# Two buffers of their own for the second quarter (b12) of the MLP's seven-product rounds

## The chip, the cores and the metric

The kernel runs on one core of one Trainium2 chip. The metric is the device time of one execution in microseconds. Three runs of the kernel before took 2303.08, 2305.74 and 2306.23 us; their median, 2305.74 us, is the time that the change is compared with.

## The reference

A decoder trunk of two layers over 256 tokens of width 2048, all in float32. Layer 0 mixes tokens with multi-head latent attention, layer 1 with a Mamba-2 scan; each mixer is followed by the same MLP, which is where the change is:

```python
def squared_relu_mlp(h, w_in, w_out):
    u = jax.nn.relu(h @ w_in)
    return (u * u) @ w_out

# in reference(), for each of the two layers
x = x + mix
h = rms_norm(x, mlp_norm_g[i])
x = x + squared_relu_mlp(h, mlp_w_in[i], mlp_w_out[i])
```

`w_in` is 2048 x 8192 and `w_out` 8192 x 2048, so each MLP reads 128 MB of weights.

## The kernel before

**Splitting.** A float32 weight is multiplied as a sum of two parts. Every piece of weights, 128 partitions x 1024 numbers (512 KB), is loaded into a raw buffer (`L85`, issued by SP). ScalarE copies it to a rounded high part `wh` (`L102`), VectorE subtracts that from the raw piece to give the low part `wl` (`L103`). TensorE multiplies high by high, low (of the activations) by high and high by low (`L615`, `L616`, `L619`). There are four `wh` and four `wl` buffers, so splitting runs at most a few units ahead of TensorE. A unit is one such piece with its products; units are numbered in the order in which TensorE consumes them, and the tile names carry that number (`wraw207`, `wl198`).

**Rounds.** The hidden width of an MLP is worked off in eight steps of 1024 columns. In steps 1 to 7 (the rounds of this text, seven in each MLP), `h @ w_in` for the step is done as a product of 2 x 2 blocks with seven products instead of eight: M1, N7, N5, N6, N4, M2, N3. The inner dimension of a block is walked in four pieces d = 0 to 3. For each d, three quarters of weights are loaded, b11 into the pool `rx`, b12 and b22 into the pool `raw`, and VectorE combines them in place (`L183`):

```python
if name == "N7":
    add("b22", "b12", "b22")
    out = halves("b22")
    ...
if name == "N5" and d not in LATE5:
    add("b12", "b11", "b12")
    return halves("b12")
if name == "N6":
    add("b11", "b11", "b22")
    out = halves("b11")
...
loads = {"M1": lambda: [load("b11", "rx", (0, 0))],
         "N7": lambda: [load("b12", B12, (0, 1)), load("b22", "raw", (1, 1))],
```

So a b12 buffer is held from its load, through the add of N7, until the split of N5. After N6 a DMA issued by GpSimd adds a further quarter onto b11 in place (`L199`). M2 and N3 load the quarter b21 or b22 again as plain pieces.

**Output.** The squared hidden columns of a round are multiplied by `w_out` in the next round, in blocks of 512 output columns with four units each (loads from `mo`). Such a block collects in a pair of PSUM banks (`yp`); at its end VectorE adds the two banks to the residual stream (`add_residual`, `L436`), and only then may the next block's first product write those banks.

**What sets the order.** TensorE's order is written out by a planner (`plan`, `merged`), which mixes the products of a round with the output units of the round before; the planner is not changed. Loads run six units ahead of TensorE inside the rounds and splits three (`self.flow.ahead`). The instructions of VectorE, ScalarE, GpSimd and SP are put into their queues by the framework's scheduler, which places each where its own estimate of durations has it start; each queue then runs strictly in that order, so an instruction that waits holds up what stands behind it. A raw load waits until the buffer that it takes has been read for the last time. Of the six `raw` buffers, a round's b12 pieces take one each while they are held.

Of the kernel before, what the change touches and what calls it, by code (L numbers as in the profile page):

```python
# [169 lines left out]
def seven(layer, p, src):  # L170
# [9 lines left out]
    def unit(flow, name, d):  # L180
# [22 lines left out]
        def load(k, pool, q):  # L203
            st[k] = Load(pool, quarter(d, *q))
            return st[k]

        loads = {"M1": lambda: [load("b11", "rx", (0, 0))],
                 "N7": lambda: [load("b12", B12, (0, 1)), load("b22", "raw", (1, 1))],
                 "M2": lambda: [load("M2", "raw", (1, 0))], "N3": lambda: [load("N3", "raw", (1, 1))]}
# [5 lines left out]
class Trunk:  # L215
# [294 lines left out]
    def mlp(self, layer, gain):  # L510
        with ExitStack() as ctx:
            mp = ctx.enter_context(self.tc.tile_pool(name="mlp", bufs=1, reuse_waits="tile"))
            for name, n in (("rx", 4), ("ry", 1)):
                self.flow.pools[name] = ctx.enter_context(self.tc.tile_pool(name=name, bufs=n, reuse_waits="tile"))
            self.flow.ahead = (4, 3)
            self.mlp_body(mp, layer, gain)
# [883 lines left out]
             "x7", "z5", "z6", "o2a", "z7", "o2b", "o3"]  # L1400


B12 = "raw"
WARM = 9
LATE5 = ()
TR = (10, 8, 7, 7, 5)
# [66 lines left out]
def sequence(d):  # L1473
# [23 lines left out]
    def mlp(i):  # L1497
# [9 lines left out]
        for nb in range(4):  # L1507
            for q in range(2):
                add(("mo", i, 7, nb, q), mo[14 + q, nb])

    mlp(0)
    col = lambda name, i: {"z": 0, "x": 8, "B": 16, "C": 18}[name] + i
    si = lambda name, i: [add(("si", name, i, q), d["si"][q, col(name, i)]) for q in range(4)]
    so = lambda k, nb: add(("so", k, nb), d["so"][k, nb])
    for step in SSM_ORDER:
# [8 lines left out]
        else:  # L1524
            for pair in ((0, 1), (2, 3)):
                for k in (6, 7):
                    for nb in pair:
                        so(k, nb)
    mlp(1)
    return seq  # L1530

# [78 lines left out]
```

## Time and profile before

| | |
|---|---|
| median of three runs | 2305.74 us |
| the profiled execution | 2303.41 us, of which the span 2301.6 us |
| TensorE busy | 2281.3 us (99%) |
| VectorE busy | 1897.7 us (82%) |
| ScalarE busy | 1391.8 us (60%) |
| HBM read | 529.65 MB, 233 GB/s read and written over the span |
| 512 KB loads into `raw` from `w_in` (`mi`), from `w_out` (`mo`) | 256 and 256, median 5.4 and 5.3 us to landing |

The profile is of one execution. Its timeline gives start, duration, engine, line, operation, tiles and, in brackets, the idle time before an instruction with what ended it; rows of equal instructions that follow each other are merged (x3). Its table of stretches gives, for each, the length and then the busy time of TensorE's matmuls, its weight loads, VectorE, ScalarE and GpSimd with their counts, the granted TensorE clock, the share of the time in which the DMA engines were busy, and GB/s. Its list of waits gives who waited for whom: total us, times, longest. Of a DMA, "to landing" is the time from its issue until its data had landed. The first MLP lies at about 275 to 925 us, the second at 1625 to 2275 us.

### The profile page before, as it was taken

Reading aid. Unit: us, or ns where it says so; the run is one execution under the profiler, and the core shown is the slowest. Engines: PE = TensorE matmul, PEld = TensorE weight load, DVE = VectorE, ACT = ScalarE, POOL = GpSimd, SP = SyncE. Lnnn points to the kernel's source line nnn. Section 1 sums busy time; section 2 is a strip of 40 time slices with the busy share of each in tenths; the row PEclk is TensorE's granted clock in tenths of the full one; section 3 lists DMA queues with packets and bytes.
Section 4 is the critical chain, followed back from the end, with each engine's and each line's share of the span. In section 5 each row is a group of like instructions: output and inputs, shape, how many; then the busy total and the mean of one; then the engine's idle time right before and its main releaser. Section 6 shows DMA issues by size and latency. Waiting matters only on the chain.

```text
span 2301.6 us, 30974 instructions
## 1 busy us (share of the span) xinstructions
PE 2281.3 (99%) x10929; PEld 1889.6 (82%) x10929; DVE 1897.7 (82%) x2290; ACT 1391.8 (60%) x1947; POOL 276.4 (12%) x315
## 2 busy tenths in 40 slices
PE   9999999999999999999999999999999999999999
PEld 7888888878878778888888888888888877878887
DVE  7786797888898888677899688677979889889884
ACT  7775566566566566564666645545666656666663
POOL 1440000000000000100133213121000000000000
PEclk9999999999999999999999999999999999999999
DMA  8545678888888878767878788767788888888874
GB/s 316 169 154 168 213 228 270 256 251 256 263 248 261 260 230 262 228 205 243 277 280 278 250 269 270 221 222 226 222 254 245 257 262 241 260 270 246 258 239 156
DMA packets 167709, 557.18 MB, mean 242 GB/s; under 512 B 19041, under 2 KB 28193, under 8 KB 166529
## 3 DMA queue, kind: packets, MB, share of 16 engines
q1 hardware_dynamic: 151264, 502.44, 66.8%
q0 software_dynamic: 13888, 48.49, 9.8%
q10 hardware_dynamic: 2400, 4.27, 0.5%
q8 instruction: 86, 1.41, 0.2%
q14 instruction: 71, 0.57, 0.1%
HBM read 529.65 MB, written 6.41 MB: 233 GB/s over the span
## 4 chain that ended last, share of the span: by engine, by line
PE 96%; DMA 2%; DVE 1%; issue 1%; ACT 0%; POOL 0%; DVEq 0%; SPq 0%; ACTq 0%
PE acc L339 13%; PE acc L340 13%; PE acc L343 13%; PE yp L615 9%; PE yp L619 9%; PE yp L616 9%; PE st L615 7%; PE st L616 7%; PE st L619 7%; DMA wraw<-mi 1%; PE sm L324 1%; PE sm L322 1%; PE y L1311 1%; PE acc L615 1%; PE acc L616 1%; PE acc L619 1%
## 5 line engine op out<-in xcount | busy, mean ns | idle before, releaser
L102 ACT ACTIVATE wh<-wraw 128x1024 fp32r<-128x1024 f32 (+1 forms) x818 | 857.8, 1054 | 604.3 <-PE acc L340 275.0
L103 DVE TENSOR_TENSOR wl<-wraw,wh 128x1024 fp32r<-128x1024 f32 (+1 forms) x818 | 984.9, 1221 | 238.0 <-ACT wh L102 225.6
L615 PE MATMUL yp<-wh,k 128*128 128x512 f32 x896 | 351.7, 393 | 12.7 <-DVE x L436 12.6
L616 PE MATMUL yp<-wh,k 128*128 128x512 f32 x896 | 349.8, 390 | 0.0
L339 PE MATMUL acc<-wh,xt 128*128 128x512 f32 x704 | 279.5, 397 | 0.5 <-ACT wh L102 0.5
L340 PE MATMUL acc<-wh,xt 128*128 128x512 f32 x704 | 274.8, 390 | 0.0
L102 ACT ACTIVATE wh<-wrx 128x1024 fp32r<-128x1024 f32 x168 | 177.7, 1060 | 136.8 <-PE yp L616 101.6
L619 PE MATMUL yp<-wl,k 128*128 128x512 f32 x896 | 239.9, 389 | 1.1 <-DVE wl L103 1.1
L103 DVE TENSOR_TENSOR wl<-wrx,wh 128x1024 fp32r<-128x1024 f32 x168 | 204.9, 1221 | 25.6 <-ACT wh L102 25.0
L615 PEld LDWEIGHTS yp<-wh,k 128*128 128x128 f32 x896 | 168.6, 188 | 53.6 <-issue 11.0
L619 PEld LDWEIGHTS yp<-wl,k 128*128 128x128 f32 x896 | 168.3, 188 | 36.6 <-DVE wl L103 1.5
L616 PEld LDWEIGHTS yp<-wh,k 128*128 128x128 f32 x896 | 168.8, 188 | 34.2
L339 PE MATMUL acc<-wh,k 128*128 128x512 f32 x496 | 196.5, 396 | 0.0
L340 PE MATMUL acc<-wh,k 128*128 128x512 f32 x496 | 193.3, 390 | 0.0
L343 PE MATMUL acc<-wl,xt 128*128 128x512 f32 x704 | 188.3, 389 | 0.0
L615 PE MATMUL st<-wh,xt 128*128 128x512 f32 x448 | 177.7, 397 | 0.0
L616 PE MATMUL st<-wh,xt 128*128 128x512 f32 x448 | 174.8, 390 | 0.0
L339 PEld LDWEIGHTS acc<-wh,xt 128*128 128x128 f32 x704 | 132.6, 188 | 29.2 <-ACT wh L102 1.4
L340 PEld LDWEIGHTS acc<-wh,xt 128*128 128x128 f32 x704 | 132.4, 188 | 28.5 <-issue 1.2
L343 PEld LDWEIGHTS acc<-wl,xt 128*128 128x128 f32 x704 | 132.2, 188 | 27.7
L619 PE MATMUL st<-wl,xt 128*128 128x512 f32 x448 | 138.0, 389 | 0.0
L199 POOL DMA_DIRECT2D wrx<-mi x56 | 49.2, 878 | 733.7 <-DVE wl L103 537.1
(319 smaller groups left out, 3464.1 us busy)
## 6 DMA issues: line engine op xcount, KB each, us to landing
wraw<-mi SPq DMA_DIRECT2D x256, 512.0 KB, 5.4
wraw<-mo SPq DMA_DIRECT2D x256, 512.0 KB, 5.3
wraw<-si SPq DMA_DIRECT2D x160, 512.0 KB, 5.2
wraw<-so SPq DMA_DIRECT2D x64, 512.0 KB, 5.5
wrx<-mi SPq DMA_DIRECT2D x56, 512.0 KB, 5.5
wrx<-mi POOLq DMA_DIRECT2D x56, 512.0 KB, 8.1
wraw<-wo SPq DMA_DIRECT2D x32, 512.0 KB, 3.9
taps<-xD SPq DMA_DIRECT2D x16, 768.0 KB, 8.2
```

The lines of the kernel that those rows point to most:

```text
L102: self.last = nc.scalar.activation(h[:, v], raw[:, v], AF.Copy)
L103: self.last_lo = nc.vector.tensor_tensor(lo[:, v], raw[:, v], h[:, v].bitcast(F32), ALU.subtract)
L199: nc.gpsimd.dma_start(st["b11"].tile, quarter(d, 1, 0), accum_op=ALU.add)
L322: self.nc.tensor.transpose(b.bitcast(F32R)[:, v], words[:, v], self.ident_r)
L324: self.nc.tensor.transpose(b[:, v], src[:, v], self.ident)
L339: nc.tensor.matmul(accs[t][:, :n], ah, wh[:, q, :], start=first and kt + q == 0, stop=False)
L340: nc.tensor.matmul(accs[t][:, :n], al, wh[:, q, :], start=False, stop=False)
L343: nc.tensor.matmul(accs[t][:, :n], lhs(kt + q, t)[0], wl[:, q, :], start=False, stop=en and q == nk - 1)
L615: nc.tensor.matmul(b, ah, half(h, q), start=first and q == 0, stop=False, skip_group_check=more)
L616: nc.tensor.matmul(b, al, half(h, q), start=False, stop=False, skip_group_check=more)
L619: nc.tensor.matmul(b, lhs(2 * kt + q, t)[0], half(lo, q), start=False, stop=last and q == 1, skip_group_check=more)
L1311: nc.tensor.matmul(y[t][c, o], part(t)[:, c], xg[g][t][:, o], start=True, stop=True)
```

## The change

A pool `rb` of two buffers of 128 x 1024 float32 (4 KB in each partition, so 8 KB more in all) is opened beside `rx` and `ry` for each MLP, and b12 is loaded into it. The six `raw` buffers serve all else as before.

```diff
@@ def mlp(self, layer, gain):
-            for name, n in (("rx", 4), ("ry", 1)):
+            for name, n in (("rx", 4), ("ry", 1), ("rb", 2)):
                 self.flow.pools[name] = ctx.enter_context(self.tc.tile_pool(name=name, bufs=n, reuse_waits="tile"))
             self.flow.ahead = (4, 3)
             self.mlp_body(mp, layer, gain)
@@
-B12 = "raw"
+B12 = "rb"
```

No instruction is added or removed. TensorE's and GpSimd's orders stay as they are; SP's, VectorE's and, in a few rows, ScalarE's change.

SP in round 3 of the first MLP, the loads around those of unit 207 (N7 of d = 3; `mi0` is the first MLP's `w_in`, `mo0` its `w_out`). Before:

```order
L85 DMA wraw198_4965<-mi0 128x1024
L85 DMA wraw198_4967<-mi0 128x1024
L85 DMA wraw199_4985<-mo0 128x1024
L85 DMA wraw202_5027<-mo0 128x1024
L85 DMA wraw203_5039<-mo0 128x1024
L85 DMA wraw204_5052<-mo0 128x1024
L85 DMA wrx227_5422<-mi0 128x1024
L85 DMA wraw207_5096<-mi0 128x1024
L85 DMA wraw207_5098<-mi0 128x1024
L85 DMA wraw210_5144<-mo0 128x1024
```

With the change:

```order
L85 DMA wraw198_4970<-mi0 128x1024
L85 DMA wrb198_4968<-mi0 128x1024
L85 DMA wraw199_4988<-mo0 128x1024
L85 DMA wraw202_5030<-mo0 128x1024
L85 DMA wraw203_5042<-mo0 128x1024
L85 DMA wrb207_5099<-mi0 128x1024
L85 DMA wraw204_5055<-mo0 128x1024
L85 DMA wraw207_5101<-mi0 128x1024
L85 DMA wrx227_5425<-mi0 128x1024
L85 DMA wraw210_5147<-mo0 128x1024
```

Both loads of 207 now stand ahead of that of `wrx227`, b12's also ahead of 204's. The load of 207's b22 takes, with the change, the buffer of 190's b22, whose last reader is the add for N6 of d = 1 (`wrx189<-wrx189,wraw190`); before, it took the buffer of 199, whose last reader is the split `wl199`.

VectorE in the same round, from split 197 to the residual adds (`x00` and `x10` are the residual stream's tiles). Before:

```order
L103 TENSOR_TENSOR wl197_5000<-wrx197_4947,wh197_4999 128x1024
L183 TENSOR_TENSOR wrx197_4947<-wrx197_4947,wraw198_4967 128x1024
L103 TENSOR_TENSOR wl198_5018<-wraw198_4967,wh198_5017 128x1024
L103 TENSOR_TENSOR wl199_5030<-wraw199_4985,wh199_5029 128x1024
L103 TENSOR_TENSOR wl200_5043<-wraw198_4965,wh200_5042 128x1024
L103 TENSOR_TENSOR wl201_5056<-wrx197_4947,wh201_5055 128x1024
L103 TENSOR_TENSOR wl202_5067<-wraw202_5027,wh202_5066 128x1024
L183 TENSOR_TENSOR wraw207_5098<-wraw207_5096,wraw207_5098 128x1024
L436 TENSOR_TENSOR x00_142<-yp_509_4945,x00_142 128x512
L436 TENSOR_TENSOR x10_146<-yp_510_4946,x10_146 128x512
```

With the change:

```order
L103 TENSOR_TENSOR wl197_5003<-wrx197_4950,wh197_5002 128x1024
L183 TENSOR_TENSOR wraw207_5101<-wrb207_5099,wraw207_5101 128x1024
L103 TENSOR_TENSOR wl198_5021<-wraw198_4970,wh198_5020 128x1024
L183 TENSOR_TENSOR wrx197_4950<-wrx197_4950,wraw198_4970 128x1024
L103 TENSOR_TENSOR wl199_5033<-wraw199_4988,wh199_5032 128x1024
L103 TENSOR_TENSOR wl200_5046<-wrb198_4968,wh200_5045 128x1024
L103 TENSOR_TENSOR wl201_5059<-wrx197_4950,wh201_5058 128x1024
L103 TENSOR_TENSOR wl202_5070<-wraw202_5030,wh202_5069 128x1024
L183 TENSOR_TENSOR wrb207_5099<-wrx206_5087,wrb207_5099 128x1024
L436 TENSOR_TENSOR x00_142<-yp_509_4948,x00_142 128x512
L436 TENSOR_TENSOR x10_146<-yp_510_4949,x10_146 128x512
```

The add for N7 of 207 moved from behind split 202 to behind split 197, and the add for N5 of the same piece from behind the residual adds to ahead of them. Rounds 4 to 6, and 2 in its last piece, change in the same way, in both MLPs; in rounds 3 to 6 the adds of d = 0, 1 and 2 keep their places.

VectorE in round 2, from split 135 (unit 140 is N7 of d = 0). Before:

```order
L103 TENSOR_TENSOR wl135_3999<-wraw135_3956,wh135_3998 128x1024
L436 TENSOR_TENSOR x02_144<-yp_466_3893,x02_144 128x512
L436 TENSOR_TENSOR x12_148<-yp_467_3894,x12_148 128x512
L300 TENSOR_TENSOR k4_464_3890<-sm_470_4016,k4_463_3889 128x4x128
L103 TENSOR_TENSOR wl136_4026<-wraw136_3968,wh136_4025 128x1024
L103 TENSOR_TENSOR wl137_4040<-wraw137_3980,wh137_4039 128x1024
L103 TENSOR_TENSOR wl138_4052<-wraw138_3996,wh138_4051 128x1024
L103 TENSOR_TENSOR wl139_4062<-wrx139_4023,wh139_4061 128x1024
L623 TENSOR_TENSOR s2_455_3774<-st_441_3377,s2_455_3774 128x512
L183 TENSOR_TENSOR wraw140_4037<-wraw140_4035,wraw140_4037 128x1024
```

With the change:

```order
L103 TENSOR_TENSOR wl135_4002<-wraw135_3959,wh135_4001 128x1024
L183 TENSOR_TENSOR wraw140_4040<-wrb140_4038,wraw140_4040 128x1024
L436 TENSOR_TENSOR x02_144<-yp_466_3896,x02_144 128x512
L436 TENSOR_TENSOR x12_148<-yp_467_3897,x12_148 128x512
L300 TENSOR_TENSOR k4_464_3893<-sm_470_4019,k4_463_3892 128x4x128
L103 TENSOR_TENSOR wl136_4029<-wraw136_3971,wh136_4028 128x1024
```

The add for N7 of 140 moved ahead of the residual adds and of splits 136 to 139.

## The prediction, as it went on record

> **What bounds the kernel now.** I read the page first, then the busy time of the two MLPs, then who waited for whom, then one round of the MLP engine by engine.
>
> ```profile
> PE 2281.3 (99%) x10929; PEld 1889.6 (82%) x10929; DVE 1897.7 (82%) x2290; ACT 1391.8 (60%) x1947; POOL 276.4 (12%) x315
> ```
> ```profile
> 275.00:925.00 650.00, 641.91 (x2897) 528.03 (x2896) 568.48 (x554) 407.20 (x441) 40.52 (x57) 1.00 0.83 252
> 925.00:1625.00 700.00, 700.00 (x3623) 577.89 (x3622) 553.63 (x742) 393.42 (x620) 129.97 (x90) 1.00 0.75 246
> 1625.00:2275.00 650.00, 643.94 (x2896) 529.71 (x2895) 566.47 (x548) 406.05 (x436) 37.59 (x52) 1.00 0.83 251
> ```
> ```profile
> PE yp L615 <- DVE x L436: 12.6, 8, 2.2
> PE yp L619 <- DVE wl L103: 1.1, 1, 1.1
> PE sm L322 <- DVE k L300: 0.4, 1, 0.4
> ...
> DVE wraw L183 <- DMA wraw<-mi: 50.9, 29, 3.7
> ```
>
> TensorE is busy 99% of the span, so no edit that leaves its matmuls alone can win more than its idle time. That idle time lies in the two MLPs, 650 - 641.91 = 8.1 us and 650 - 643.94 = 6.1 us; the SSM between them has none. The waits say how it arises: eight times, 12.6 us in all, the first matmul of an output block waited for the residual add (L436) that empties its bank; VectorE in turn stood 50.9 us, 29 times, at an add of raw weights (L183) whose load had not landed.
>
> Round 3 shows the link. VectorE's timeline, then TensorE's:
>
> ```profile
> 496.87 1.22 DVE L183 TENSOR_TENSOR wrx<-wrx,wraw 128x1024 f32<-128x1024 f32 x1
> ...
> 502.55 1.22 DVE L103 TENSOR_TENSOR wl<-wrx,wh 128x1024 fp32r<-128x1024 f32 x1
> 503.81 1.22 DVE L183 TENSOR_TENSOR wrx<-wrx,wraw 128x1024 f32<-128x1024 f32 x1
> 504.95 3.49 DVE L103 TENSOR_TENSOR wl<-wraw,wh 128x1024 fp32r<-128x1024 f32 x3
> ...
> 509.49 1.22 DVE L103 TENSOR_TENSOR wl<-wraw,wh 128x1024 fp32r<-128x1024 f32 x1
> 514.21 1.22 DVE L183 TENSOR_TENSOR wraw<-wraw,wraw 128x1024 f32<-128x1024 f32 x1 [3.50 <-DMA wraw<-mi]
> 515.35 1.28 DVE L436 TENSOR_TENSOR x<-yp,x 128x512 f32<-128x512 f32 x2
> ```
> ```profile
> 513.39 0.61 PE L619 MATMUL st<-wl,sN 128*128 128x512 f32 x2
> 516.18 0.47 PE L615 MATMUL yp<-wh,k 128*128 128x512 f32 x1 [2.17 <-DVE x L436]
> ...
> 519.07 0.39 PE L615 MATMUL yp<-wh,k 128*128 128x512 f32 x1
> ```
>
> VectorE has no idle time from 502.55 to 510.7 (no row has a bracket), then stands 3.50 us before the add of unit 207, with the two residual adds queued behind it. TensorE was ready at 516.18 - 2.17 = 514.01 and lost 2.17 us. The 207 loads were late since the last of them took the buffer of load 199, whose split is the second of the three from 504.95 (ends 507.3).
>
> **The change part by part.** It adds no instruction; it moves b12 out of the six `raw` buffers and so shifts when loads may start and where the scheduler puts the adds.
>
> *Loads.* With both b12 loads elsewhere, the b22 load of 207 takes the buffer of 190's b22, last read by the add that starts at 496.87 (ends 498.1). SP's rows before it wait for splits that end earlier, so it issues at about 498.1, not 507.3. A load (then 204's) did issue there. Its landing, and the worst of its like, round 4's:
>
> ```profile
> L85 SPq DMA_DIRECT2D wraw<-mo x1: 328/328/328, 498.1 to 498.1; - x1
> ...
> DMA to landing us min/median/max: 6.0/6.0/6.0
> ```
> ```profile
> L85 SPq DMA_DIRECT2D wraw<-mo x1: 328/328/328, 583.5 to 583.5; - x1
> ...
> DMA to landing us min/median/max: 7.9/7.9/7.9
> ```
>
> In the steady rounds 3 to 6 of both MLPs that slot's eight landings take 6.0, 7.9, 6.7, 6.3 and 6.9, 6.9, 6.8, 6.2 us, mean 6.7. The bytes and the times of issue stay, so I take these values. The bounds are the page's medians below and the 8.2 us of a load that ran beside an accumulating one (its row is at the third rival).
>
> ```profile
> wraw<-mi SPq DMA_DIRECT2D x256, 512.0 KB, 5.4
> wraw<-mo SPq DMA_DIRECT2D x256, 512.0 KB, 5.3
> ```
>
> *VectorE.* The scheduler also moves the add of 207 ahead, from after split 202 to after split 197 (starts 502.55, so the next can start at 503.7), and N5's add of 207 to before the residual adds. VectorE now arrives 503.7 - 498.1 = 5.6 us after the load is issued and waits 6.0 + 0.1 - 5.6 = 0.5 us, not 3.50; over the eight rounds 0.5, 2.4, 1.2, 0.8 and 1.4, 1.4, 1.3, 0.7 us. The residual adds follow two adds of 1.14 us (the distance of starts) and that wait after 510.7: 510.7 + 2.28 + 0.5 = 513.5 against 515.35. TensorE starts 516.18 - 515.35 = 0.83 us after them, 0.15 more for the second bank: 514.5, still 0.5 us after 514.01, if VectorE comes no earlier.
>
> It does. The first add of the round stood 1.56 us:
>
> ```profile
> 464.03 2.06 SPq L85 DMA_DIRECT2D wraw<-mi  x2
> ```
> ```profile
> 469.46 0.68 DVE L300 TENSOR_TENSOR k<-sm,k 128x512 fp32r<-128x512 f32 x1
> 471.70 1.23 DVE L183 TENSOR_TENSOR wraw<-wraw,wraw 128x1024 f32<-128x1024 f32 x1 [1.56 <-DMA wraw<-mi]
> ```
> ```profile
> 498.22 1.06 ACT L102 ACTIVATE wh<-wrx 128x1024 fp32r<-128x1024 f32 x1 [1.71 <-PE yp L616]
> ```
>
> The two loads of that add went at 464.0 and, with 0.33 us for the last issue, at 464.03 + 2.06 - 0.33 = 465.8; the second now takes the first's place, 1.7 us earlier, and the wait nearly goes. The lead passes down VectorE's unbroken queue until something not on VectorE stops it: split 196, which started at 500.28, needs the ScalarE copy above, done at 499.28 and held by TensorE. So 1.0 us survives, in each steady round, since the limit is TensorE's. A round then loses its wait less 1.0: 0, 1.4, 0.2, 0, 0.4, 0.4, 0.3, 0, together 2.7 us.
>
> Split 198 now stands behind the add; it is done at 504.95 + 1.2 = 506.2 and TensorE takes it 1.8 us later (its first low product at 507.95). One add of 1.14 and 0.5 us of wait, less the lead, fit.
>
> *Round 2 of each MLP* had no gap and can get one. The add of 140 moves from 391.27 to ahead of the residual adds at 384.18:
>
> ```profile
> 382.33 1.23 DVE L103 TENSOR_TENSOR wl<-wraw,wh 128x1024 fp32r<-128x1024 f32 x1
> 384.18 1.29 DVE L436 TENSOR_TENSOR x<-yp,x 128x512 f32<-128x512 f32 x2 [0.63 <-PE yp L619]
> 385.39 0.68 DVE L300 TENSOR_TENSOR k<-sm,k 128x512 fp32r<-128x512 f32 x1
> 385.99 3.49 DVE L103 TENSOR_TENSOR wl<-wraw,wh 128x1024 fp32r<-128x1024 f32 x3
> ```
> ```profile
> L85 SPq DMA_DIRECT2D wraw<-mi x1: 328/328/328, 380.9 to 380.9; - x1
> ...
> DMA to landing us min/median/max: 5.3/5.3/5.3
> ```
> ```profile
> 389.59 0.62 PE L619 MATMUL st<-wl,xt 128*128 128x512 f32 x2
> ```
>
> (The last row is unit 136's low products.) The b22 load goes at 380.9, lands at 386.2; the add runs 386.3 to 387.5, the residual adds from 387.4, L300 at 388.6, split 136 from 389.2 to 390.4. TensorE wants it at 389.59: 0.9 us lost, twice, 1.8 us.
>
> *Round 7 and the clock.* Round 7 lost 1.1 us behind a wait of 3.74; its load, one place earlier, leaves about 1.9, and I keep 0.2 of its 1.1 + 0.4 us in gaps.
>
> ```profile
> 814.57 1.23 DVE L183 TENSOR_TENSOR wraw<-wraw,wraw 128x1024 f32<-128x1024 f32 x1 [3.74 <-DMA wraw<-mi]
> ```
> ```profile
> 1859.90 0.63 PE L615 MATMUL yp<-wh,k 128*128 128x512 f32 x1 [2.15 <-DVE x L436]
> ```
> ```profile
> 1860.00:1865.00 5.00, 5.00 (x15) 3.92 (x16) 5.00 (x6) 1.06 (x1) 0.00 (x0) 0.66 0.76 215
> ```
>
> After the 2.15 us gap the granted clock was 0.66 for 5 us, 0.34 x 5 = 1.7 us lost. Each gap also costs 0.17 us of slow restart (516.18 to 519.07 is 2.89 us for twelve matmuls, 12 x 0.227 = 2.72 without a gap). By the Trainium skill (TensorE: Matmul & The Clock Gate, HAM oscillation) the clock falls only for idle gaps beyond some 3.4 us; the row has it fall after 2.15. By that rule the clock is no term and the sum below comes out 1.7 us smaller.
>
> *Sum.* Gone: 14.1 us of gaps (12.6 + 1.1 + 0.4), 8 x 0.17 = 1.4 of restarts, 1.7 of clock, together 17.2. Left or new: 2.7 + 1.8 + 0.2 + 7 restarts of 0.17 = 1.2, together 5.9. Net 11.3 us. The early b12 loads (two go out in the attention stage, two in the SSM stage) I put at nothing: they delay the loads behind them by one issue each, and in TensorE's waits no load of those stages appears.
>
> The profiled execution took 2303.41 us, span 2301.6 and 1.8 around it: it becomes 2292.1. The median of the runs is 2305.74, 2.3 above it: 2294.4.
>
> **The rivals.**
>
> *Every gap goes.* If loads land in about 5.6 us, as the page's medians have it (5.3 and 5.4), no wait exceeds the lead: the time falls by 17.2 to 2288.5. Against it: the slot's own mean is 6.7, loads going out four in a row. The Trainium skill says the like (Perfetto Trace Analysis, Optimization Strategy): consistent bubbles can mean too little room for the next tile. More room would end them by that.
>
> *VectorE's queue is the limit, not the buffers.* Two adds now stand ahead of the residual adds that stood partly behind. If the 1.0 us lead does not survive, the rounds keep their waits, 9.7 us, with 1.8 + 0.2 + 1.7 + 1.7 for the rest: 15.1 against 17.2, so 2303.6, no change to be seen. For it: VectorE is without idle time through these stretches. Against it: the 1.56 us wait.
>
> *Slower: the wait now stops split 198.* The add stands before five splits that TensorE consumes. If the slot lands as slowly as the load issued at 486.6, beside an accumulating one,
>
> ```profile
> L85 SPq DMA_DIRECT2D wraw<-mi x1: 328/328/328, 486.6 to 486.6; - x1
> ...
> DMA to landing us min/median/max: 8.2/8.2/8.2
> ```
>
> each wait is 8.2 + 0.1 - 5.6 = 2.7, less 1.0, in eight rounds 13.6; round 2 loses 0.9 + 2.9 twice, 7.6; restarts and a clock step 3.4: 24.6, or 7.4 us slower, 2313. It decides from 7.4 us of landing on, where 8 x (7.4 - 6.5) + 2 x (7.4 - 4.4) + 3.4 = 16.6 is about what is gone. DMA's share of 0.83 speaks for it; against, the same issue times with mean 6.7. The Trainium skill (DMA: Bandwidth & Descriptors, Issuing engines are not separate DMA queues) has all loads interleave on the same sixteen engines, which would lengthen each.
>
> **How the numbers follow.** Forecast 0.60, all gaps gone 0.18, no change 0.13, slower 0.09. Within 0.2% is within 4.6 us. So faster 0.78, within 0.13, slower 0.09. The range runs from 2287 (17.2 off the profiled execution is 2286.2, off the median 2288.5) to 2303, into the case of no change; about 0.17 lies above it, 0.03 below.
>
> **What would show it.** In the changed profile: the VectorE wait at L183 falls from 50.9 us to 15 to 25; in steady rounds the only one left is 0.5 to 2.4 us before the fourth piece's add, now ahead of split 198; TensorE's wait for L436 falls to 2 to 4 us; round 2 shows a new wait of TensorE for L103 of about 0.9 us. It is wrong if that slot's landing exceeds 7.4 us, if the waits for L436 stay near 12, or if waits for L103 take their place in rounds 3 to 6.

## The result, and the profile after

The changed kernel took 2290.78 us (median of 6 runs, 2288.99 to 2294.92), the kernel before 2303.87 us (median of 6, 2298.93 to 2306.23). The ratio is 0.995, with a 95% interval from 0.9935 to 0.9965: 13.1 us faster. The profiled execution took 2290.86 us with a span of 2289.1, which is 12.5 us less than the span before. The forecast was 2294.4 us, from 2287 to 2303.

The page's line of busy times, the stretches of the two MLPs and the waits, all of the changed kernel:

```profile
PE 2278.0 (100%) x10929; PEld 1888.7 (83%) x10929; DVE 1894.6 (83%) x2290; ACT 1393.0 (61%) x1947; POOL 275.2 (12%) x315
```
```profile
275.00:925.00 650.00, 647.58 (x2927) 534.21 (x2926) 571.69 (x558) 411.49 (x445) 41.30 (x58) 1.00 0.83 254
...
1625.00:2275.00 650.00, 647.67 (x2923) 533.87 (x2922) 565.73 (x549) 407.91 (x437) 37.50 (x52) 1.00 0.81 248
```
```profile
PE yp L615 <- DVE x L436: 2.7, 3, 1.2
PE st L619 <- DVE wl L103: 2.0, 2, 1.3
...
DVE wraw L183 <- DMA wraw<-mi: 20.1, 18, 3.3
```

TensorE's idle time in the MLPs is 2.42 + 2.33 = 4.75 us, where it was 14.15: 9.4 of the 12.5 us. TensorE's busy time fell by 3.3 us (2281.3 to 2278.0), and 0.2 us more idle time stands outside the MLPs. 1.7 of the 3.3 us are the clock, which is 1.00 in every 5 us of both MLPs now; that the rest are the slow matmuls after gaps is the forecast's reading, and no run shows it by itself. VectorE's wait for raw weights fell from 50.9 to 20.1 us.

Round 3 of the first MLP again: VectorE, then TensorE, then the load of 207's b22.

```profile
504.73 1.23 DVE L183 TENSOR_TENSOR wraw<-wrb,wraw 128x1024 f32<-128x1024 f32 x1 [0.38 <-DMA wraw<-mi]
505.87 1.22 DVE L103 TENSOR_TENSOR wl<-wraw,wh 128x1024 fp32r<-128x1024 f32 x1
...
513.82 1.28 DVE L436 TENSOR_TENSOR x<-yp,x 128x512 f32<-128x512 f32 x2
```
```profile
515.38 0.39 PE L615 MATMUL yp<-wh,k 128*128 128x512 f32 x1
```
```profile
L85 SPq DMA_DIRECT2D wraw<-mi x1: 328/328/328, 498.3 to 498.3; - x1
...
DMA to landing us min/median/max: 6.4/6.4/6.4
```

The load went out at 498.3, where the load of the same tile had gone at 507.3. The add of 207 stands ahead of split 198, waits 0.38 us instead of 3.50, and the output block's first matmul has no bracket: the gap of 2.17 us is gone.

What is left lies in rounds 2 and 7 of both MLPs and in one steady round. Round 2 of the first MLP, VectorE and TensorE:

```profile
387.12 1.23 DVE L183 TENSOR_TENSOR wraw<-wrb,wraw 128x1024 f32<-128x1024 f32 x1 [3.27 <-DMA wraw<-mi]
388.26 1.28 DVE L436 TENSOR_TENSOR x<-yp,x 128x512 f32<-128x512 f32 x2
```
```profile
391.33 0.74 PE L619 MATMUL st<-wl,xt 128*128 128x512 f32 x2 [1.28 <-DVE wl L103]
```

Round 7, VectorE and TensorE after, then VectorE before:

```profile
840.11 1.23 DVE L183 TENSOR_TENSOR wraw<-wrb,wraw 128x1024 f32<-128x1024 f32 x1 [1.99 <-DMA wraw<-mi]
...
843.52 1.28 DVE L436 TENSOR_TENSOR x<-yp,x 128x512 f32<-128x512 f32 x2
```
```profile
844.35 0.47 PE L615 MATMUL yp<-wh,k 128*128 128x512 f32 x1 [1.13 <-DVE x L436]
```
```profile
849.69 1.28 DVE L436 TENSOR_TENSOR x<-yp,x 128x512 f32<-128x512 f32 x2
...
859.41 1.23 DVE L183 TENSOR_TENSOR wraw<-wraw,wraw 128x1024 f32<-128x1024 f32 x1 [1.63 <-DMA wraw<-mi]
```

And round 5 of the second MLP, the only steady round with a gap:

```profile
2008.84 1.22 DVE L183 TENSOR_TENSOR wraw<-wrb,wraw 128x1024 f32<-128x1024 f32 x1 [1.67 <-DMA wraw<-mi]
```
```profile
2018.76 0.47 PE L615 MATMUL yp<-wh,k 128*128 128x512 f32 x1 [0.40 <-DVE x L436]
```

The gaps are 1.28 and 0.73 us in round 2 (2.01), 1.13 and 1.20 in round 7 (2.33), and 0.40: 4.74 in all. The four of rounds 2 and 7 stand behind an N7 add that the scheduler had moved ahead of the residual adds. In the steady round the N7 add was ahead of them before as well; there it moved ahead of five splits, and N5's add moved ahead of the residual adds.

### The profile page after: what moved, and what is told of

It is laid out like the page before. It is cut to its first block, busy times and chain, and to the rows that moved or that the text cites. A ratio compares the mean times of both kernels' runs of the same rounds, so it can differ in the third digit from the quotient of the medians.

```text
span 2289.1 us, 30981 instructions
## 1 busy us (share of the span) xinstructions
PE 2278.0 (100%) x10929; PEld 1888.7 (83%) x10929; DVE 1894.6 (83%) x2290; ACT 1393.0 (61%) x1947; POOL 275.2 (12%) x315
## 4 chain that ended last, share of the span: by engine, by line
PE 98%; DMA 1%; DVE 1%; issue 0%; ACT 0%; POOL 0%; SPq 0%; DVEq 0%; ACTq 0%
PE acc L339 13%; PE acc L340 13%; PE acc L343 13%; PE yp L615 9%; PE yp L616 9%; PE yp L619 9%; PE st L619 8%; PE st L615 8%; PE st L616 8%; PE sm L324 1%; PE sm L322 1%; PE y L1311 1%; PE acc L615 1%; PE acc L616 1%; PE acc L619 1%; PE acc L727 0%
## 5 line engine op out<-in xcount | busy, mean ns | idle before, releaser
L102 ACT ACTIVATE wh<-wraw 128x1024 fp32r<-128x1024 f32 (+2 forms) x762 | 798.5, 1053 | 562.2 <-PE acc L340 276.0
L103 DVE TENSOR_TENSOR wl<-wraw,wh 128x1024 fp32r<-128x1024 f32 (+2 forms) x762 | 920.3, 1221 | 234.8 <-ACT wh L102 219.4
```

The source lines that it names most:

```text
L102: self.last = nc.scalar.activation(h[:, v], raw[:, v], AF.Copy)
L103: self.last_lo = nc.vector.tensor_tensor(lo[:, v], raw[:, v], h[:, v].bitcast(F32), ALU.subtract)
```

## The experiments

The forecast had one cause in it, *room*: with two more buffers the load goes out early enough. But the change does two things at once. The load goes earlier, and the scheduler then moves the add ahead, past splits and past the residual adds. The rival theory is *place*: what costs is that something TensorE wants stands behind an add that waits for a load, and moving the add back would do as well as the buffers. A third, *own ring*, is that the long-lived b12 blocks the short-lived tiles that share its ring (the buffers of one pool). Every kernel here computes the whole MLP; only buffers and the order differ. The ratios are to the kernel before, timed beside them: 2302.45 us beside the eight buffers by turns, the two forms with the adds held back that follow it, and the two buffers withheld; 2304.67 us beside the other four. In the diffs "..." stands for lines left out.

**Eight buffers shared by turns.** b12 goes back to the common ring, and every fourth raw load of an MLP takes one of the two extra buffers:

```diff
+        if self.turns and ld.pool == "raw" and self.units[self.loaded].key[0] in ("s", "c", "o"):
+            self.turn += 1
+            if self.turn % 4 == 0:
+                ld.pool = "rb"
...
-B12 = "rb"
+B12 = "raw"
```

> The same two extra buffers, but not kept for b12: b12 goes back to the six, and every fourth raw load of the MLP, whatever it is, takes one of the two. Theory 'room' (eight buffers in all let the b22 load go out some 9 us earlier, whichever tiles they hold): as the change, 2289 to 2293 us, VectorE's wait for raw loads near 20 us. Theory 'own ring' (b12 lives long and blocks the short-lived tiles behind it, and it is its removal that counts): at least half of the 13 us gain goes, 2297 us or more, and the wait for raw loads is 35 us or more.

Measured: 2303.53 us, ratio 1.0 (0.9988 to 1.0011). Nothing was gained. The waits of TensorE, of its weight loads and of VectorE (here the split is L108, the raw add L188, the residual add L441, the low products L626), and the start of round 4 on VectorE and TensorE:

```profile
PE yp L622 <- DVE x L441: 5.7, 5, 1.7
PE st L626 <- DVE wl L108: 2.8, 4, 1.1
```
```profile
PEld st L626 <- DVE wl L108: 12.6, 21, 1.5
```
```profile
DVE wraw L188 <- DMA wraw<-mi: 23.5, 12, 2.9
DVE wrb L188 <- DMA wrb<-mi: 15.0, 6, 3.3
```
```profile
552.74 1.23 DVE L188 TENSOR_TENSOR wraw<-wraw,wraw 128x1024 f32<-128x1024 f32 x1 [2.94 <-DMA wraw<-mi]
553.88 1.28 DVE L441 TENSOR_TENSOR x<-yp,x 128x512 f32<-128x512 f32 x2
555.08 1.22 DVE L108 TENSOR_TENSOR wl<-wraw,wh 128x1024 fp32r<-128x1024 f32 x1
```
```profile
556.35 0.73 PE L626 MATMUL st<-wl,xt 128*128 128x512 f32 x2 [0.72 <-DVE wl L108]
```

By the numbers this was the result that *own ring* had expected: 38.5 us of waits for raw loads, and no gain. But the rows show something else: the add of d = 0 now stands ahead of the residual adds and of the split that TensorE takes next, and waits 2.94 us there. The loss does not show as idle time: that fell to 6.03 + 3.45 = 9.48 us in the MLPs, from 14.15, while TensorE's busy time rose to 2283.9 us, from 2281.3. Where the busy time grew is not shown row by row; the weight loads' 21 waits for splits, 12.6 us, are the likely place. In the changed kernel the same add stands behind them:

```profile
551.91 2.35 DVE L103 TENSOR_TENSOR wl<-wraw,wh 128x1024 fp32r<-128x1024 f32 x2
...
555.48 1.23 DVE L183 TENSOR_TENSOR wraw<-wrb,wraw 128x1024 f32<-128x1024 f32 x1 [0.61 <-DMA wraw<-mi]
```

So eight buffers in all are not enough by themselves, which refutes *room* in its plain form; ring or place was still open.

**The change with the adds held back.** The scheduler may issue the add of N7 only after the split of the unit four places before it, which puts it behind the residual adds. The loads go out as in the change.

```diff
+        self.los.append(self.last_lo)
...
-                add("b22", "b12", "b22")
+                with flow.after(flow.los[-4]) if True else nullcontext():
+                    add("b22", "b12", "b22")
...
+        self.flow.after = lambda i: self.tc.issue_after(i.ins)
```

`los` collects VectorE's splits in order, and `after` has the scheduler place the add behind the split that it is given.

> The change with every N7 add held back until the split of the unit four places before it has been issued, so that it stands behind the residual adds; the loads go out as in the change. Theory 'room' (the early load saves the time, the early place of the add costs): the gaps that the change left in round 2 (2.0 us) and round 7 (2.3 us) and the 0.4 us go, TensorE's wait for the residual adds falls below 1 us, VectorE's wait for raw loads below 5 us, 2286 to 2287.5 us. Theory 'queue' (the new early place of the adds saves the time): gaps come back in the steady rounds, 2297 us or more.

Measured: 2283.72 us, ratio 0.9912 (0.9898 to 0.9927), an interval wholly below that of the change. The MLPs, and VectorE's wait for raw weights:

```profile
275.00:925.00 650.00, 650.00 (x2948) 537.48 (x2947) 577.87 (x562) 413.96 (x449) 41.30 (x58) 1.00 0.83 255
...
1625.00:2275.00 650.00, 650.00 (x2947) 537.75 (x2946) 568.22 (x549) 405.25 (x434) 37.50 (x52) 1.00 0.81 248
```
```profile
DVE wraw L185 <- DMA wraw<-mi: 3.1, 8, 0.6
```

TensorE shows no idle time in either MLP, and the time is below what either theory had. The early place of the adds was no part of the gain; it cost the change 7.1 us (2290.86 less 2283.72 by the profiled executions), of which 4.75 are the gaps above. The rest, 2.4 us, is more than the expectation had: 2.0 of it is in TensorE's busy time (2278.0 us in the change, 2276.0 here), and no run says in which rows.

**The kernel before with the adds held back.** The same hold, in the kernel before, with six buffers for everything.

```diff
-                add("b22", "b12", "b22")
+                with flow.after(flow.los[-4]) if True else nullcontext():
+                    add("b22", "b12", "b22")
```

> The kernel before, with its six buffers for everything, and only the same holding back of every N7 add, to behind the residual adds. Theory 'room' (the late load itself costs, wherever the add stands): no more than a third of the gain, 2299 us or more, with TensorE waiting for splits in place of residual adds. Theory 'place in the queue' (a late load costs only because the residual adds stand behind the add that waits for it): the gaps go without any buffer, 2286 to 2291 us, with VectorE's wait for raw loads below 25 us and TensorE's wait for the residual adds below 3 us.

Measured: 2285.73 us, ratio 0.9921 (0.9907 to 0.9935): 16.7 us gained with no buffer at all, more than the change gained. The first MLP (in the second TensorE is busy all 650.00 us), the wait for raw weights, round 3 on VectorE (the residual add is L439 here), and the load of 207's b22:

```profile
275.00:925.00 650.00, 649.23 (x2943) 536.62 (x2942) 575.39 (x561) 412.71 (x448) 41.31 (x58) 1.00 0.83 256
```
```profile
DVE wraw L185 <- DMA wraw<-mi: 15.7, 14, 2.2
```
```profile
510.57 1.29 DVE L439 TENSOR_TENSOR x<-yp,x 128x512 f32<-128x512 f32 x2 [0.63 <-PE yp L623]
...
515.30 1.22 DVE L185 TENSOR_TENSOR wraw<-wraw,wraw 128x1024 f32<-128x1024 f32 x1
```
```profile
L86 SPq DMA_DIRECT2D wraw<-mi x1: 328/328/328, 506.5 to 506.5; - x1
...
DMA to landing us min/median/max: 6.4/6.4/6.4
```

The load is as late as ever (506.5), but the residual adds no longer stand behind its add: they now wait for TensorE, not TensorE for them. This decides for *place* here: what the late load had cost was the work behind the add that waits for it.

**The early load with the old place.** The change with the hold one unit earlier (five places instead of four). In rounds 3 to 6 the add of d = 3 then stands where the kernel before has it, behind split 202 and ahead of the residual adds.

```diff
-                add("b22", "b12", "b22")
+                with flow.after(flow.los[-5]) if True else nullcontext():
+                    add("b22", "b12", "b22")
```

> The change with its early loads, but every N7 add held back until the split of the unit five places before it, which in rounds 3 to 6 puts the add of d = 3 where the kernel before has it: behind split 202 and ahead of the residual adds (round 2 keeps the order of the change). So only the loads differ from before there. Theory 'room' (the early load alone ends the wait): in rounds 3 to 6 the add meets its landed load, no gap of TensorE is left there, the 2.0 us of round 2 stay, 2287 to 2291 us. Theory 'place' (the old place costs, whenever the load goes out): the gaps for the residual adds of rounds 3 to 6 come back, 2298 us or more.

Measured: 2286.44 us, ratio 0.9928 (0.9917 to 0.994). TensorE's wait and the add in round 3:

```profile
PE st L623 <- DVE wl L104: 2.1, 2, 1.2
```
```profile
511.40 1.22 DVE L185 TENSOR_TENSOR wraw<-wrb,wraw 128x1024 f32<-128x1024 f32 x1
```

The row has no bracket: the add meets a load that has landed, and no gap is left but the two of round 2, whose order is that of the change. In round 7 the hold puts the add of d = 3 back behind the residual adds, and the gaps of the change are gone there. So *room* holds as well where the add stays put: either remedy ends the waits of the steady rounds. The Trainium skill (Perfetto Trace Analysis, Optimization Strategy) names too little room for the next tile as what consistent bubbles can mean; these two runs agree with the "can": the same bubbles went with more room (2286.44) and without it (2285.73).

**Eight buffers by turns, adds held back.** Both edits above together.

> The eight buffers shared by turns (of which nothing was gained: 2303.5 us), and now with every N7 add held back until the split of the unit four places before it has been issued. Theory 'place' (the loss of the shared form lies in the adds of d = 0, which stood ahead of the split that TensorE wants next and waited 2.2 to 3.3 us there): TensorE's weight loads stop waiting for splits (12.6 us before, below 1 us now), VectorE's waits for raw loads fall from 38.5 to below 20 us, 2283.5 to 2286 us. Theory 'own ring' (b12 kept with the others delays the loads themselves): TensorE waits on, 2294 us or more.

Measured: 2283.76 us, ratio 0.9916 (0.9903 to 0.9929), within 0.1 us of the form in which b12 has its own two. VectorE waited for raw loads 0.3 us in all:

```profile
DVE wrb L190 <- DMA wrb<-mi: 0.3, 1, 0.3
```

The whole of what the shared form had lost was the place of its adds: TensorE's weight loads no longer wait for splits in the MLPs, and its busy time is 2276.0 us, from 2283.9. *Own ring* falls: once the adds are held, nothing in the time depends on which tiles share the eight buffers.

**Two of the six withheld.** The change, with two tiles taken from the six at the start of an MLP and given back at its end, so that b12 keeps its two and all else shares four.

```diff
+            held = [self.flow.pools["raw"].tile([P, 1024], F32, tag="raw", name=self.name("held")) for _ in range(2)]
+            for h in held:
+                self.nc.gpsimd.memset(h[:, :16], 0.0)
             self.mlp_body(mp, layer, gain)
+            for h in held:
+                self.nc.gpsimd.tensor_copy(self.stat(16), h[:, :16])
```

> The change with two of the six buffers withheld during each MLP: b12 has its own two, all else shares four, six in all as before. Theory 'room': nothing of the gain is left, 2302 us or more, TensorE's wait for the residual adds is 10 us or more. Theory 'own ring': half of the gain or more stays, 2297 us or less.

Measured: 2315.23 us, ratio 1.0046 (1.003 to 1.0061). The two MLPs, and GpSimd at the start of the second:

```profile
275.00:925.00 650.00, 635.74 (x2839) 518.56 (x2838) 561.46 (x545) 393.29 (x434) 40.26 (x56) 0.99 0.81 245
...
1625.00:2275.00 650.00, 647.78 (x2933) 534.65 (x2932) 573.82 (x562) 412.51 (x446) 39.80 (x58) 1.00 0.82 251
```
```profile
1634.84 1.19 POOL L521 COPY st<-held 128x16 f32<-128x16 f32 x2
```

The edit worked in the first MLP only: in the second the scheduler gave the two tiles back at 1634.84, ten microseconds into the stage. So the run is its own comparison. With six buffers in the MLP TensorE lost 14.26 us, with eight 2.22 us, about what the change loses there (2.33): where the adds are not held, room counts, as *room* expected by the time. The wait for the residual adds, for which it had 10 us or more, was 6.8. Another 7.0 of the 14.26 us were waits for splits: the longest, 2.47 us at 572.20, was for a split behind an add that had waited 2.03 us for its load. So this run does not part the late load from the place of its add. A fixed pair for b12 out of six is worse than six shared (8.09 us in that MLP before).

**One buffer for b12.** `("rb", 2)` becomes `("rb", 1)`; nothing is held back.

> One buffer for b12 instead of two, the six as they are. The b12 load of a piece then waits until the product N5 of the piece before has been split, and stands in SP's queue meanwhile; the scheduler puts the add of d = 3 behind split 205, and keeps that of round 2 ahead of the residual adds. Theory 'place': steady rounds without gaps, round 2 with its 2 us, 2284 to 2289 us. Theory 'room': loads behind the blocked one go out as late as before or later, VectorE waits 40 us or more for raw loads, 2300 us or more.

Measured: 2309.26 us, ratio 1.0022 (1.0013 to 1.0031). VectorE's wait for b12, and its worst case for TensorE, in round 1 of the first MLP on VectorE and TensorE:

```profile
DVE wraw L183 <- DMA wrb<-mi: 45.8, 27, 3.3
```
```profile
340.58 1.22 DVE L183 TENSOR_TENSOR wraw<-wrb,wraw 128x1024 f32<-128x1024 f32 x1 [2.70 <-DMA wrb<-mi]
```
```profile
342.94 0.50 PE L615 MATMUL st<-wh,sN 128*128 128x512 f32 x1 [3.12 <-ACT wh L102]
```

The number is the one *room* expected; the mechanism is not. The load that comes late is b12's own, for which the one buffer has to come free, and TensorE then waits for the unit that the add makes, not for work behind the add: ScalarE's copy of the sum is done at 342.9, one copy after the add. The second MLP has the same gap of 2.92 us at 1687.04. In rounds 3 to 6 no gap exceeds 0.3 us, as *place* had it; but its total was wrong by some 20 us, since it did not ask when the unit itself is due. Each MLP lost some 7 us of TensorE's time (643.32 and 642.88 us busy of 650).

**Five buffers, adds held back.** The kernel before with `pool("raw", 5)` in the whole kernel, and the hold.

> The kernel before with five raw buffers instead of six in the whole kernel, and the adds held back to four splits before. With six, the last load of a round landed at 514 us for an add that then ran at 515.3; one buffer less puts that load one split (1.2 us) to one unit (5 us) later. Theory 'place' (room has slack once nothing TensorE wants stands behind the add): gaps below 6 us in all, 2284 to 2292 us. Theory 'room': every buffer counts, TensorE loses 20 us or more, 2305 us or more.

Measured: 2291.92 us, ratio 0.9952 (0.994 to 0.9964): one buffer fewer than before, and as fast as the change with two more. The two MLPs and the SSM stage between them:

```profile
275.00:925.00 650.00, 649.07 (x2941) 536.21 (x2940) 574.55 (x559) 408.67 (x447) 41.31 (x58) 1.00 0.82 256
925.00:1625.00 700.00, 696.67 (x3595) 574.21 (x3594) 550.93 (x740) 389.56 (x615) 125.00 (x88) 1.00 0.73 244
1625.00:2275.00 650.00, 647.83 (x2924) 534.16 (x2923) 569.02 (x550) 405.39 (x438) 37.49 (x52) 1.00 0.82 252
```

The MLPs lost 3.10 us, less than with the change; 3.33 more went in the SSM stage, which had lost nothing with six. That is 6.4 us in all, a little over the 6 that *place* had allowed and far from the 20 of *room*.

**The order of merit** is 2283.7 us with the hold and two more buffers, shared or not, 2285.7 with the hold alone and 2286.4 with the buffers and the adds of rounds 3 to 6 in their old place (these two are not told apart: 2284.14 to 2288.57 and 2286.20 to 2287.93), 2290.8 for the change as it stands, 2291.9 with five buffers and the hold. The other three forms gained nothing or lost. Three of the forms with the hold came out 0.3 to 2.3 us below the range of the theory that held for them. The first beats both kernels, and in its MLPs TensorE shows no idle time.

## Why the prediction was right, and where it was not

*What bounds the kernel: right.* The gaps were the residual adds behind an add of raw weights, and taking that away, by the hold alone, took all but 0.77 us of the MLPs' idle time (a wait for another row).

*The loads: right.* The b22 load of 207 went at 498.3 (forecast 498.1). The slot's eight landings took 6.4, 6.3, 7.3, 6.7 and 6.2, 6.1, 7.6, 5.9 us, mean 6.6 against 6.7.

*The steady rounds: right in mechanism, the term mis-sized.* The forecast kept 2.7 us of gaps; 0.40 were left. Two of its numbers were too pessimistic. The waits were 0.38, 0.77, 1.27, 0.75 and 0.23, 0.44, 1.67, 0 us, together 5.5 where it had 9.7: in round 3 VectorE came to the add 6.05 us after the load was issued (504.73 - 0.38 - 498.3), not 5.6, so that a load had longer to land. And the lead that no wait uses up was not 1.0 us: a wait of 1.27 us made no gap, one of 1.67 made 0.40, so it is about 1.27. Some 0.15 of the difference is a term of the working, "0.15 more for the second bank": where TensorE did wait for the residual adds in the changed kernel, it started 0.83 us after them (844.35 - 843.52, 2018.76 - 2017.93), without the 0.15.

*Round 2: right.* A wait of TensorE for the split of 1.28 and 0.73 us, 2.01 for the 1.8 forecast, at the place named. The runs with the hold show that it was the price of the add's early place, not of the buffers: the gaps go with the adds held behind the residual adds, and stay with the hold one unit earlier, which leaves round 2 as in the change.

*Round 7: wrong.* "Its load, one place earlier, leaves about 1.9, and I keep 0.2": it kept 2.33 us. The step looked at the add of d = 0, which now waits 1.26 and 0.93 us without a gap. The gap comes from the add of d = 3, which stood behind the residual adds before (859.41 against 849.69) and now stands ahead of them (840.11 against 843.52), as in round 2. The forecast had named this move for rounds 2 to 6, and did not look for it in round 7.

*Restarts and clock: the clock right, the rest too small.* Beside the gaps 3.1 us were gained; the forecast had 1.4 + 1.7 gone and 1.2 new, 1.9 net. The clock did not fall in the changed MLPs, as the sum had it. The form without any gap shows the full size: TensorE's busy time fell by 5.3 us there (2281.3 to 2276.0), where the forecast's restarts and clock come to 3.1. What the other 2.2 us are stays open.

*The sum: right to 1.2 us by the spans, in part by luck.* The 11.3 us forecast and the 12.5 measured differ by 2.3 kept too much in the steady rounds, 2.1 too little in round 7, 0.2 too little in round 2, and 1.2 more gained in the busy time: the two largest errors nearly cancel. The median is off by more, 2290.78 against 2294.4, since the forecast set it 2.3 us above the profiled execution, as in the three runs that it knew; in the six runs of the changed kernel it was 0.1 below (2290.86).

*The rivals.* That every gap goes was within reach, but not by more room: it took the hold. That VectorE's queue is the limit and nothing changes falls. That the wait would stop split 198 did not happen: the one landing over 7.4 us, of 7.6, cost 0.40 us. But its mechanism is real: in the form shared by turns the add of d = 0 stood ahead of a split that TensorE wanted, and took back the whole gain. What the forecast did not weigh at all is that the move of the adds was itself a term, of 7.1 us to the bad, and that holding them back needs no buffer.

## What to carry to other kernels

When an engine that works strictly in its queue's order waits for a load, with work behind it that the bounding engine wants, look first at whether the waiting instruction need stand there: holding it back gained 16.7 us here with no memory, two buffers of 512 KB each gained 13.1. If room is added, read the new order for every place at which the scheduler uses it to move the consumer ahead, since each of them can hand the gain back; one form with the same eight buffers gained nothing until its adds were held.

## What was not expected of the hardware

TensorE's clock is not told by the length of a gap alone. In the kernel with two tiles withheld a gap of 2.05 us was followed by a lower granted clock; in the one with one buffer for b12 a gap of 2.92 us was not. For each, the matmul with its gap, then the stretches of 3.41 us around it, whose limits the next paragraph explains:

```profile
784.10 0.47 PE L620 MATMUL yp<-wh,k 128*128 128x512 f32 x1 [2.05 <-DVE x L436]
```
```profile
781.76:785.17 3.41, 1.36 (x6) 0.78 (x5) 3.04 (x4) 1.12 (x2) 0.00 (x0) 1.00 0.82 193
785.17:788.58 3.41, 3.41 (x10) 2.67 (x9) 3.41 (x4) 1.06 (x1) 0.00 (x0) 0.50 0.97 302
```
```profile
1687.04 0.50 PE L615 MATMUL st<-wh,sN 128*128 128x512 f32 x1 [2.92 <-ACT wh L102]
```
```profile
1682.21:1685.62 3.41, 1.91 (x11) 1.39 (x9) 0.95 (x1) 0.00 (x0) 0.00 (x0) 1.00 0.94 167
1685.62:1689.03 3.41, 1.88 (x7) 1.26 (x8) 3.38 (x4) 3.10 (x4) 0.00 (x0) 1.00 0.13 25
```

Inside the MLPs and the SSM stage the traces of this case have five drops of the clock, each to 0.50 for 3.41 us (1.7 us lost, as the forecast priced it). The two drops of the kernel with two tiles withheld begin at 573.54 and 785.17, 211.63 us apart, which is 62 lengths of 3.413 us. Lay out each trace in stretches of that length, counted from a change of its clock. In all five cases the stretch that ends where the drop begins held 2.05 to 2.47 us of TensorE's idle time, and no stretch without a drop behind it held more than 1.66 us. The gap of 2.92 us fell across a limit, 1.50 us on one side and 1.42 on the other. In the kernel before, the gap of 2.15 us lay whole in one stretch (1856.63 to 1860.04), while those of 2.17 us (at 516.18) and 2.24 us (at 2032.01) were divided and cost no clock. This is read from ten traces after the fact, and no run was made to test it.

The Trainium skill (TensorE: Matmul & The Clock Gate, HAM oscillation) has the clock fall for idle gaps beyond some 3.4 us; the first pair disagrees, as the 2.15 us gap of the kernel before did.
